# Sliding windows of a 2D image batch: another order of the loads, fewer split stores, and the last two stores back on the common queue

## The chip, the cores and the metric

The kernel runs on one core of one Trainium2 chip. The metric is the device time of one execution in microseconds; the figure for a kernel is the median of its runs. The profile is of one execution, and its times count from that execution's first instruction.

## The reference

The input `x` is a float32 array of 16 x 64 x 64 x 64 (batch, channel, height, width). For each of 15 x 15 window positions (8 x 8 windows, stride 4) the window of all channels is copied out. Nothing is computed; the output holds every input element about four times.

```python
for i in range(n_h):
    for j in range(n_w):
        h_start = i * stride
        w_start = j * stride
        result[:, i, j] = x[:, :, h_start:h_start + window_size, w_start:w_start + window_size].copy()
```

The output is 16 x 15 x 15 x 64 x 8 x 8 float32, 58.98 MB; the input is 16.78 MB. So 75.76 MB have to be moved.

## The kernel before, in words

**Layout.** The 128 partitions are (batch 16) x (channel half 2) x (height quarter 4). Each partition holds 32 channels (CL) of 16 rows (RB) by 64 columns, in one tile `L` (L45). A window position is a pair (j, s): j is the column position (15 of them), s one of four row slots within the partition's 16 rows (NSLOT). Because all four height quarters are worked at once, one pair (j, s) covers four rows of windows, or three for s = 3, where the quarter at the bottom has no window. There are 60 pairs, in `order` (L82), j outermost.

**Loads.** The channels are loaded in NCH = 4 parts of 8 channels (L49 to L54). Each part is four DMAs, one for each height quarter, alternating between the SP and ACT queues: 16 DMAs of 1,024 KB. The first half of a partition's channels is parts 0 and 1.

**Copies.** For each pair, `window` gathers the strided window of every partition into a contiguous store buffer. For s = 0 to 2 this is one copy on ACT (L111). For s = 3 the lower half of the window lies in the next partition, so DVE copies the upper four rows (L113) and fetches the lower four with a shuffle across partitions (L114).

**Store buffers.** `G` (L94) is a list of nine tiles, each of 18 / 2 units; a unit is a half window (16 channels, 512 KB over all partitions), a tile holds a whole one (1,024 KB). The counter `at` goes round the 18 units.

**Stores.** Each buffer leaves by an indirect DMA that POOL issues (L124): an index for each partition (`idx`, or `idx_last` for s = 3; `idx_h` and `idx_hlast` for half windows) gives the row of the output, and an index beyond the bound, for the bottom quarter at s = 3, is left out. All stores are declared independent of one another (`free`, L88). At most eight of them are under way: the next waits until the one eight places before it in the queue has landed. A copy into a tile waits until the store that last read the tile has landed.

**Order.** The first EARLY = 12 pairs are split: their first half (channels of parts 0 and 1) is copied and stored as soon as these parts are there (L136). Then second halves and whole windows alternate, two and two (L140 to L145), and whole windows follow (L146).

**The last two pairs.** The pairs in `order[-TAIL:]`, TAIL = 2, are stored by plain DMAs on the SP queue (L115 to L119), one for each height quarter: four for (14, 2), three for (14, 3), 256 KB each. Ahead of them the counter is set back by three tiles (L148, BACK = 3), so they use tiles again whose stores were issued last but two and last but one.

Of the kernel before, what the change touches and what calls it, by code (L numbers as in the profile page):

```python
# [1 line left out]

# [4 lines left out]


@with_exitstack  # L10
def kernel(
    ctx: ExitStack,
    tc: tile.TileContext,
    x: bass.AP,
    window_size: int,
    stride: int,
    out: bass.AP,
):
    nc = tc.nc
    P = nc.NUM_PARTITIONS  # L20

    B, C, H, W = x.shape
    Bo, NH, NW, Co, WSo, WSo2 = out.shape
    WS = int(window_size)
    ST = int(stride)
    assert Bo == B and Co == C and WSo == WS and WSo2 == WS

    f32 = mybir.dt.float32
    i32 = mybir.dt.int32
    ALU = mybir.AluOpType  # L30
    HQ = 4
    CH = P // (B * HQ)
    CL = C // CH
    RB = H // HQ
    NSLOT = RB // ST
    NWIN = NH * NW
    CFREE = CL * WS * WS
    assert HQ == 4 and CH == 2 and WS == 2 * ST

    lpool = ctx.enter_context(tc.tile_pool(name="lpool", bufs=1))  # L40
    ipool = ctx.enter_context(tc.tile_pool(name="ipool", bufs=1))
    gpool = ctx.enter_context(tc.tile_pool(name="gpool", bufs=1))


    L = lpool.tile([P, CL, RB, W], f32)  # L45
    x_v = x.rearrange("b (ch cl) (hq r) w -> hq (b ch) cl (r w)", ch=CH, hq=HQ)
    NCH = 4
    cw = CL // NCH
    for k in range(NCH):  # L49
        for q in range(HQ):  # L50
            (nc.sync, nc.scalar)[q % 2].dma_start(
                out=L[q::HQ, k * cw : (k + 1) * cw, :, :],
                in_=x_v[q, :, k * cw : (k + 1) * cw, :],
            )  # L54


    def itile(name):
        return ipool.tile([P, 1], i32, name=name)

    pi, tb, tq, tc_, idx, idx_last = (itile(n) for n in ("pi", "tb", "tq", "tc", "idx", "idx_last"))  # L60
    nc.gpsimd.iota(pi[:, :], pattern=[[0, 1]], base=0, channel_multiplier=1)  # L61
    nc.vector.tensor_scalar(out=tb[:, :], in0=pi[:, :], scalar1=3, scalar2=None, op0=ALU.logical_shift_right)  # L62
    nc.vector.tensor_scalar(out=tc_[:, :], in0=pi[:, :], scalar1=2, scalar2=1, op0=ALU.logical_shift_right, op1=ALU.bitwise_and)  # L63
    nc.vector.tensor_scalar(out=tq[:, :], in0=pi[:, :], scalar1=HQ - 1, scalar2=None, op0=ALU.bitwise_and)  # L64
    nc.vector.tensor_scalar(out=tb[:, :], in0=tb[:, :], scalar1=float(NWIN * CH), scalar2=None, op0=ALU.mult)  # L65
    nc.vector.tensor_tensor(out=tb[:, :], in0=tb[:, :], in1=tc_[:, :], op=ALU.add)  # L66
    nc.vector.tensor_scalar(out=tc_[:, :], in0=tq[:, :], scalar1=float(NSLOT * NW * CH), scalar2=None, op0=ALU.mult)  # L67
    nc.vector.tensor_tensor(out=idx[:, :], in0=tb[:, :], in1=tc_[:, :], op=ALU.add)  # L68

    nc.vector.tensor_scalar(out=tq[:, :], in0=tq[:, :], scalar1=float(HQ - 1), scalar2=float(2 * B * NWIN * CH), op0=ALU.is_equal, op1=ALU.mult)  # L70
    nc.vector.tensor_tensor(out=idx_last[:, :], in0=idx[:, :], in1=tq[:, :], op=ALU.add)  # L71


    HCL = CL // 2
    idx_h, idx_hlast = itile("idx_h"), itile("idx_hlast")
    for d, e in ((idx_h, idx), (idx_hlast, idx_last)):
        nc.vector.tensor_scalar(out=d[:, :], in0=e[:, :], scalar1=2.0, scalar2=None, op0=ALU.mult)  # L77
    o_v = out.rearrange("b i j (ch cl) r w -> (b i j ch) (cl r w)", ch=CH)
    o_h = out.rearrange("b i j (ch cl) r w -> (b i j ch) (cl r w)", ch=2 * CH)
    nxt = [min(p + 1, 31) for p in range(32)]  # L80

    order = [(j, s) for j in range(NW) for s in range(NSLOT)]  # L82


    TAIL, BACK = 2, 3
    o_q = out.rearrange("b i j (ch cl) r w -> i j b ch (cl r w)", ch=CH)

    def free(st):  # L88
        tc.declare_no_dep(st.ins, group="stores", reason="each store writes rows of its own")
        tc.add_to_no_dep_group("stores", st.ins)  # L90


    UNITS = 18
    G = [gpool.tile([P, 2 * HCL, WS, WS], f32, name=f"G{n}") for n in range(UNITS // 2)]  # L94
    at = 0

    def window(j, s, half):
        nonlocal at
        cols = slice(j * ST, j * ST + WS)
        last = s == NSLOT - 1  # L100
        if half is None:
            n, c0 = 2, 0
            at += at % 2
        else:
            n, c0 = 1, half * HCL
        u = at % UNITS
        at += n
        cs = slice(c0, c0 + n * HCL)
        g = G[u // 2][:, u % 2 * HCL : (u % 2 + n) * HCL, :, :]
        if not last:  # L110
            nc.scalar.copy(out=g, in_=L[:, cs, s * ST : s * ST + WS, cols])  # L111
        else:
            nc.vector.tensor_copy(out=g[:, :, 0:ST, :], in_=L[:, cs, s * ST : RB, cols])  # L113
            nc.vector.stream_shuffle(out=g[:, :, ST:WS, :], in_=L[:, cs, 0:ST, cols], mask=nxt)  # L114
        if (j, s) in order[-TAIL:]:  # L115
            g_q = g.rearrange("(m q) c r w -> q m (c r w)", q=HQ)
            for q in range(HQ - 1 if last else HQ):
                free(nc.sync.dma_start(out=o_q[q * NSLOT + s, j], in_=g_q[q]))
            return  # L119
        if half is None:  # L120
            o, ix = o_v, (idx_last if last else idx)
        else:
            o, ix = o_h, (idx_hlast if last else idx_h)
        st = nc.gpsimd.indirect_dma_start(  # L124
            out=o,
            out_offset=bass.IndirectOffsetOnAxis(ap=ix[:, 0:1], axis=0),
            in_=g.rearrange("p c r w -> p (c r w)"),
            in_offset=None,
            element_offset=(s * NW + j) * CH * CFREE + (half or 0) * HCL * WS * WS,
            bounds_check=B * NWIN * CH * (1 if half is None else 2) - 1,  # L130
            oob_is_err=False,
        )
        free(st)

    EARLY = 12
    for j, s in order[:EARLY]:  # L136
        window(j, s, 0)
    late = list(order[:EARLY])
    rest = list(order[EARLY:])
    while late:  # L140
        for w in late[:2]:
            window(*w, 1)
        for w in rest[:2]:
            window(*w, None)
        late, rest = late[2:], rest[2:]  # L145
    for w in rest[:-TAIL]:  # L146
        window(*w, None)
    at -= 2 * BACK  # L148
    for w in rest[-TAIL:]:
        window(*w, None)  # L150


# [1 line left out]
_INS = ['x', 'window_size', 'stride']  # L154
_OUTS = [((16, 15, 15, 64, 8, 8), 'float32')]

_NUMBERS = {'window_size': 8, 'stride': 4}


# [26 lines left out]
```

## Time and profile before

| | us |
|---|---|
| median of 3 runs | 193.19 |
| range of the runs | 192.94 to 193.51 |
| the profiled execution's own time | 193.19 |
| its span, first to last instruction | 191.4 |
| ACT busy | 86.2 (45%) |
| POOL busy | 68.0 (36%) |
| DVE busy | 30.4 (16%) |
| packets of the indirect stores, share of 16 DMA engines | 73.3% (57.15 MB) |
| packets of the SP queue (8 loads, 7 stores) | 13.8% (10.22 MB) |
| packets of the ACT queue (8 loads) | 11.1% (8.39 MB) |

The mean time of one instruction: 1,896 ns for an ACT copy of a whole window and 1,040 ns for a half; 694 and 1,280 ns for DVE's copy and shuffle of a whole window; some 965 ns for POOL's issue of a store. The busy time of POOL on a store is the issue alone; the bytes move afterwards. From issue to landing the profile gives a median of 18.4 us for whole windows and 14.1 us for half windows on POOL's queue, 4.2 us for SP's stores, and 21.1 and 19.8 us for the loads on SP's and ACT's queues. The DMA share of a stretch can read a little over 1 because packets overlap.

### The profile page before, as it was taken

To read this page: it belongs to the slowest core of one execution; us is meant where nothing else is said; L and a number is where in the kernel's file an instruction comes from. 1 tells how busy PE (TensorE), PEld (TensorE's weight loads), DVE (VectorE), ACT (ScalarE), POOL (GpSimd) and SP (SyncE) were. 2 spreads that over 40 slices of the span, in tenths; PEclk is the share of its full clock that TensorE was granted. 3 is DMA by queue.
4 is the path that set the end of the run, shared out by engine and by line. 5 is a ranking of instruction groups with operands and counts; after the bars stand their busy time and mean duration, and the time that the engine had idled before them with its cause. 6 is when DMAs were issued, how large, how long until landed. Compare 5 with 4: busy or idle time off the path is not lost.

```text
span 191.4 us, 479 instructions
## 1 busy us (share of the span) xinstructions
DVE 30.4 (16%) x65; ACT 86.2 (45%) x55; POOL 68.0 (36%) x75
## 2 busy tenths in 40 slices
DVE  2000050000232302301221031203030303000030
ACT  0000059400699876364566556565647473300300
POOL 0000028723367666464464343434444444400000
DMA  5999999999999999999999999999999999999785
GB/s 180 419 413 410 410 409 413 416 423 420 417 423 429 423 418 425 407 406 414 410 413 404 414 416 413 404 409 409 411 407 409 411 409 406 416 411 416 325 265 187
DMA packets 14772, 75.80 MB, mean 396 GB/s; under 512 B 2032, under 2 KB 2032, under 8 KB 9008
## 3 DMA queue, kind: packets, MB, share of 16 engines
q0 software_dynamic: 10080, 57.15, 73.3%
q1 hardware_dynamic: 2512, 10.22, 13.8%
q10 hardware_dynamic: 2176, 8.39, 11.1%
q14 instruction: 4, 0.03, 0.0%
HBM read 16.78 MB, written 62.65 MB: 415 GB/s over the span
## 4 chain that ended last, share of the span: by engine, by line
DMA 73%; issue 19%; ACT 2%; POOL 1%; DVE 1%; POOLq 0%; DVEq 0%; PEldq 0%; ACTq 0%
DMA out_dram<-G,idx 60%; DMA out_dram<-G,idx_h 13%; ACT G L111 2%; POOL out_dram L124 1%; DVE G L114 1%; DVE G L113 0%; POOLq L124 0%; POOL pi L61 0%; DVEq L113 0%; PEldq L181 0%; ACTq L111 0%
## 5 line engine op out<-in xcount | busy, mean ns | idle before, releaser
L111 ACT COPY G<-L 128x2048 f32<-128x2048 f32 (+1 forms) x54 | 84.9, 1611 | 69.1 <-DMA out_dram<-G,idx_last 25.1
L124 POOL DMA_INDIRECT out_dram<-G,idx x35 | 33.8, 966 | 45.9 <-DMA out_dram<-G,idx 41.7
L113 DVE COPY G<-L 128x1024 f32<-128x1024 f32 (+1 forms) x18 | 11.1, 614 | 152.1 <-DMA out_dram<-G,idx 76.5
L124 POOL DMA_INDIRECT out_dram<-G,idx_h x18 | 17.4, 964 | 13.9 <-DMA out_dram<-G,idx_hlast 4.8
L114 DVE STREAM_SHUFFLE G<-L 128x1024 f32<-128x1024 f32 (+1 forms) x18 | 19.6, 1091 | 0.0
L124 POOL DMA_INDIRECT out_dram<-G,idx_hlast x6 | 5.9, 989 | 27.8 <-DVE G L114 26.3
L124 POOL DMA_INDIRECT out_dram<-G,idx_last x11 | 10.6, 964 | 10.6 <-DVE G L114 5.8
L111 ACT ACT_TABLE_LOAD x1 | 1.3, 1283 | 25.9 <-DMA L<-in_x_dram 25.9
L62 DVE TENSOR_SCALAR tb<-pi 128x1 int32<-128x1 int32 x1 | 0.2, 154 | 1.0 <-POOL pi L61 1.0
L61 POOL IOTA pi<- 128x1 int32 x1 | 0.1, 119 | 0.4 <-PEq L181 0.4
L114 DVE LOAD_MASK_SELECT G<-L x18 | 0.2, 12 | 0.0
L167 POOL MEMSET const-float32-0.0<- 128x1 f32 x1 | 0.1, 98 | 0.2 <-issue 0.2
L66 DVE CUSTOM_DVE_ANT_0 tb<-tb,tc 128x2 uint16<-128x2 uint16 x1 | 0.2, 160 | 0.0
L68 DVE CUSTOM_DVE_ANT_0 idx<-tb,tc 128x2 uint16<-128x2 uint16 x1 | 0.2, 158 | 0.0
L67 DVE TENSOR_SCALAR tc<-tq 128x1 int32<-128x1 int32 x1 | 0.2, 153 | 0.0
L77 DVE TENSOR_SCALAR idx_hlast<-idx_last 128x1 int32<-128x1 int32 x1 | 0.2, 153 | 0.0
L77 DVE TENSOR_SCALAR idx_h<-idx 128x1 int32<-128x1 int32 x1 | 0.2, 154 | 0.0
L71 DVE CUSTOM_DVE_ANT_0 idx_last<-idx,tq 128x2 uint16<-128x2 uint16 x1 | 0.2, 153 | 0.0
L65 DVE TENSOR_SCALAR tb<-tb 128x1 int32<-128x1 int32 x1 | 0.2, 151 | 0.0
L70 DVE TENSOR_SCALAR tq<-tq 128x1 int32<-128x1 int32 x1 | 0.1, 147 | 0.0
L64 DVE TENSOR_SCALAR tq<-pi 128x1 int32<-128x1 int32 x1 | 0.1, 144 | 0.0
L63 DVE TENSOR_SCALAR tc<-pi 128x1 int32<-128x1 int32 x1 | 0.1, 143 | 0.0
(3 smaller groups left out, 0.3 us busy)
## 6 DMA issues: line engine op xcount, KB each, us to landing
L<-in_x_dram SPq DMA_DIRECT2D x8, 1024.0 KB, 21.1
L<-in_x_dram ACTq DMA_DIRECT2D x8, 1024.0 KB, 19.8
out_dram<-G SPq DMA_DIRECT2D x7, 256.0 KB, 4.2
out_dram<-G,idx POOLq DMA_INDIRECT x35, 18.4
out_dram<-G,idx_h POOLq DMA_INDIRECT x18, 14.1
out_dram<-G,idx_last POOLq DMA_INDIRECT x11, 18.4
out_dram<-G,idx_hlast POOLq DMA_INDIRECT x6, 11.9
```

Source lines behind the costliest of these rows:

```text
L61: nc.gpsimd.iota(pi[:, :], pattern=[[0, 1]], base=0, channel_multiplier=1)
L62: nc.vector.tensor_scalar(out=tb[:, :], in0=pi[:, :], scalar1=3, scalar2=None, op0=ALU.logical_shift_right)
L65: nc.vector.tensor_scalar(out=tb[:, :], in0=tb[:, :], scalar1=float(NWIN * CH), scalar2=None, op0=ALU.mult)
L66: nc.vector.tensor_tensor(out=tb[:, :], in0=tb[:, :], in1=tc_[:, :], op=ALU.add)
L67: nc.vector.tensor_scalar(out=tc_[:, :], in0=tq[:, :], scalar1=float(NSLOT * NW * CH), scalar2=None, op0=ALU.mult)
L68: nc.vector.tensor_tensor(out=idx[:, :], in0=tb[:, :], in1=tc_[:, :], op=ALU.add)
L71: nc.vector.tensor_tensor(out=idx_last[:, :], in0=idx[:, :], in1=tq[:, :], op=ALU.add)
L77: nc.vector.tensor_scalar(out=d[:, :], in0=e[:, :], scalar1=2.0, scalar2=None, op0=ALU.mult)
L111: nc.scalar.copy(out=g, in_=L[:, cs, s * ST : s * ST + WS, cols])
L113: nc.vector.tensor_copy(out=g[:, :, 0:ST, :], in_=L[:, cs, s * ST : RB, cols])
L114: nc.vector.stream_shuffle(out=g[:, :, ST:WS, :], in_=L[:, cs, 0:ST, cols], mask=nxt)
L124: st = nc.gpsimd.indirect_dma_start(out=o, out_offset=bass.IndirectOffsetOnAxis(ap=ix[:, 0:1], axis=0), in_=g.rearrange("p c r w -> p (c r ...
```

## The change

The four parts of the channels are loaded in the order 2, 0, 1, 3, so the first half of the channels (parts 0 and 1) comes second and third. EARLY is 8 in place of 12: eight pairs are split into halves, and four more pairs are stored whole. TAIL, BACK, the seven plain stores on SP and the setting back of the counter are gone: the last two pairs are stored by POOL's indirect DMAs like all others, from the tiles that are next in turn. What `free` did is written in its place.

```diff
-    for k in range(NCH):
+
+    for k in (2, 0, 1, 3):
         for q in range(HQ):
             (nc.sync, nc.scalar)[q % 2].dma_start(
...
-    TAIL, BACK = 2, 3
-    o_q = out.rearrange("b i j (ch cl) r w -> i j b ch (cl r w)", ch=CH)
-
-    def free(st):
-        tc.declare_no_dep(st.ins, group="stores", reason="each store writes rows of its own")
-        tc.add_to_no_dep_group("stores", st.ins)
-
...
-        if (j, s) in order[-TAIL:]:
-            g_q = g.rearrange("(m q) c r w -> q m (c r w)", q=HQ)
-            for q in range(HQ - 1 if last else HQ):
-                free(nc.sync.dma_start(out=o_q[q * NSLOT + s, j], in_=g_q[q]))
-            return
...
-        free(st)
+        tc.declare_no_dep(st.ins, group="stores", reason="each store writes rows of its own")
+        tc.add_to_no_dep_group("stores", st.ins)
 
-    EARLY = 12
+    EARLY = 8
     for j, s in order[:EARLY]:
         window(j, s, 0)
...
-    for w in rest[:-TAIL]:
-        window(*w, None)
-    at -= 2 * BACK
-    for w in rest[-TAIL:]:
+    for w in rest:
         window(*w, None)
```

## The prediction

> **What bounds the kernel now.** I read the page first: how busy the DMA engines are, and the chain that ended last.
>
> ```profile
> span 191.4 us, 479 instructions
> ...
> DMA  5999999999999999999999999999999999999785
> GB/s 180 419 413 410 410 409 413 416 423 420 417 423 429 423 418 425 407 406 414 410 413 404 414 416 413 404 409 409 411 407 409 411 409 406 416 411 416 325 265 187
> ...
> DMA 73%; issue 19%; ACT 2%; POOL 1%; DVE 1%; POOLq 0%; DVEq 0%; PEldq 0%; ACTq 0%
> ```
>
> No compute engine is over 45% busy, while the DMA engines are full from the second of the 40 slices to the 37th. The kernel moves bytes at 404 to 429 GB/s and is late only at its two ends. What matters is therefore (a) whether the DMA engines ever run out of work, (b) at what rate they move it, and (c) how the last bytes leave. I then asked for the rate by stage (columns: stretch, its length, busy time and number of instructions on DVE, ACT and POOL, clock, DMA share, GB/s).
>
> ```profile
> 4.00:25.00 21.00, 0.00 (x0) 0.00 (x0) 0.00 (x0) 1.00 1.02 412
> 30.00:49.00 19.00, 0.00 (x0) 5.80 (x7) 9.60 (x10) 1.00 1.03 419
> 50.00:60.00 10.00, 2.62 (x6) 10.00 (x9) 6.57 (x7) 1.00 1.03 423
> ...
> 100.00:160.00 60.00, 12.34 (x21) 34.15 (x18) 23.88 (x25) 1.00 1.01 410
> 160.00:179.50 19.50, 0.49 (x1) 4.08 (x3) 3.09 (x4) 1.00 1.01 414
> 179.50:182.00 2.50, 0.27 (x1) 1.61 (x1) 0.00 (x0) 1.00 0.51 213
> 182.00:189.50 7.50, 1.62 (x3) 0.00 (x0) 0.00 (x0) 1.00 0.87 282
> ```
>
> Loads alone run at 412, loads beside half-stores at 419, half-stores and the first whole ones at 423, whole stores alone at 410 to 414. From 179.5 us the rate halves and never recovers. The timeline there tells why, and the chain of waits gives the pace of the stores before it (start, length, what).
>
> ```profile
> 165.95 0.96 POOL L124 DMA_INDIRECT out_dram<-G,idx  x1 [1.50 <-DMA out_dram<-G,idx]
> 179.21 1.90 ACT L111 COPY G<-L 128x2048 f32<-128x2048 f32 x1 [14.52 <-DMA out_dram<-G,idx_last]
> 181.14 6.21 SPq L118 DMA_DIRECT2D out_dram<-G  x7
> 181.73 0.69 DVE L113 COPY G<-L 128x1024 f32<-128x1024 f32 x1 [21.24 <-DMA out_dram<-G,idx]
> ```
>
> ```profile
> 124.37 18.75 DMA out_dram<-G,idx
> ...
> 143.88 18.84 DMA out_dram<-G,idx
> ...
> 163.49 18.12 DMA out_dram<-G,idx
> ```
>
> POOL issues its last store at 165.95. The copy for the next-to-last window waits 14.52 us for a buffer, because the counter was set back by three tiles, onto a tile whose store is still queued; the last window waits 21.24 us in the same way. SP issues its seven plain stores from 181.14 on, when the queue of indirect stores is running dry. In the chain, each store is issued when the one eight before it lands. Landings are at 124.37 + 18.75 = 143.12, then 162.72, then 181.61: eight windows (six whole, two of three quarters, so 7.5 whole stores) take 19.60 and 18.89 us, or 2.61 and 2.52 us for one whole store, 1.96 and 1.89 us for a last row.
>
> **The change, part by part.**
>
> *The tail.* Removed: the setting back of the counter, and seven SP stores of 256 KB (1.84 MB in all). Added: two indirect stores on POOL, 0.96 us of issue each (L124). They take the next free tiles, so the copies no longer wait 14.52 and 21.24 us but, like every window before them, for the store nine back; and the issue waits for the store eight back. In the timeline the stores issued at 149.03 and 151.01 are those two; at 18.7 us to land and some 0.75 us to the next issue (162.72 to 163.49 in the chain) the new stores go out near 168.5 and 170.5, with more than ten microseconds of queue before them. So they simply follow in the queue. The store issued at 163.49 lands at 181.61; after it come the one of 165.95, the new whole one and the new last-row one: 2 x 2.52 + 1.89 = 6.93 us at the better pace, 2 x 2.61 + 1.96 = 7.18 at the worse, so the last byte lands at 188.5 to 188.8. Before, SP's last issue is at 186.2 and its median landing 4.2 us later, so 190.4. The tail is worth 1.6 to 1.9 us; I take 1.7, nearer the pace that held for most of the run. The close from the last landing to the end of the span (191.4 - 190.4 = 1.0 us) waits for all queues in both kernels and stays.
>
> The Trainium skill, in "DMA: Bandwidth & Descriptors", section "Issuing engine by pattern", sends a simple store to Sync and says HWDGE is generally faster; that speaks against this part. Here the plain stores got 282 GB/s (182 to 189.5) and the indirect ones 410 to 414, so the row disagrees for stores of 256 KB issued one after another. By the page the removal would cost, by the row it gains, and I go by the row.
>
> *The load order.* Sixteen load DMAs of 1,024 KB go out as before, on the same queues; only which part they carry changes. The first copies need parts 0 and 1, which in the old order are the first eight DMAs, landed when ACT's wait ends at 25.89; in the new order twelve are needed. Four more are 4.19 MB, at 412 GB/s 10.2 us: 36.1. The first store, 1.38 us after the loads in the old kernel (27.27 against 25.89), goes out at 37.5. This costs nothing only while loads keep the engines full. All loads alone would last 16.78 MB / 412 = 40.7 us from about 2.3, to 43; from about 39 the stores take a share. With loads running, POOL's waits for a free slot end at 40.23, 43.98 and 47.29, so a half-store (0.52 MB or 0.39) lands each 3.5 us: a third of the rate. The last 1.7 MB of loads then take some 6 us, to 45, in place of 49.6. Half-stores issued from 37.5 on at one per 1.27 us (31.22, 32.49, 33.76 in the timeline) are seven by then, 3.4 MB, of which 0.85 has gone: 2.5 MB are queued, 6 us of cover. The next supply: the second halves' copies start at 45, take 1.04 us each on ACT, and POOL stores them from 47.7 on. The cover of 6 us is over twice the 2.7 needed, so the hole is priced at nothing; with no cover it would be 2.7 plus about 2 us from issue to first bytes, some 4.7.
> What does cost is the rate: some 12 us that ran mixed at 419 now run as loads alone at 412, 12 x 7/412 = 0.2 us; from 0, if mixing only shifts what is moved when, to 0.4 if it is doubled by the slower start.
>
> *Eight split windows in place of twelve.* Four windows of 3.93 MB leave as four stores in place of eight, so POOL issues four fewer (3.9 us of an engine that is 36% busy, hidden under the DMA). The transfer: 3.93 MB at 423 is 9.3 us, at 410 it is 9.6; so 0 to 0.3 us lost. The first whole stores ran in the fast stage too, so I take 0.1. Copies on ACT and DVE shrink by their fixed part (two of 1.04 against one of 1.90), hidden.
>
> The same page's section "Bandwidth" asks for at least 1 MiB per DMA, by which dropping halves of 0.5 MB would gain. The stages here say 423 with halves and 410 without, so nothing is booked as a gain.
>
> *The buffers.* The list of nine tiles is the same text in both versions; nothing to cost. Declaring the stores independent moves into the function, with no instruction.
>
> **The sum.** 191.4 - 1.7 + 0.2 + 0.1 = 190.0 us of span. The profiled execution took 193.19 us, 1.8 over its span, and is itself the median of the three runs. 190.0 + 1.8 = 191.8 us. If paces and rates take their good ends, 191.4 - 1.9 + 1.8 = 191.3; at their bad ends, 191.4 - 1.6 + 0.4 + 0.3 + 1.8 = 192.3.
>
> **The rivals.**
> 1. *Slower: the pace of the stores falls.* The place is the long stage of whole stores from about 55 us to the end. Its cycle was 18.89 us once and 19.60 otherwise; at 423 GB/s 7.86 MB would take 18.6, so the pace already moves by a microsecond for reasons that the page doesn't show. The new stage starts some 10 us earlier and there are no other DMAs at its end to use engines that finish early: the halved rate at 179.5 shows that some finish well before others. If the cycle is 20.2 in place of 19.6, the 6.8 cycles from 55 to 188 add 4.1 us: 195.9. It decides, against the 1.4 us forecast, from 0.3 us a cycle on (2 us in all). For it: the rate did fall when halves ended. Against it: the bytes and their places are the same, and the last cycle was the fastest.
> 2. *No change.* If the spread of the engines' ends, at least the 2.5 us for which the rate was halved, is a fifth wider at the new last store (my choice of size), that is 0.5 us more; if the load order and the whole stores each cost their bad end too, 0.4 + 0.3, then 191.4 - 1.6 + 1.2 + 1.8 = 192.8.
> 3. *A hole after the loads.* If the first stores got no share of the engines before 45 us and were slow to start, the 4.7 us worked out above appear as a dip near 45 to 50 us: 191.8 + 4.7 = 196.5. Against it: in the old kernel stores landed beside the loads all the time, and seven or eight are queued.
> 4. *The reordering does more than it says:* the early stage without half-stores could be faster. If the whole-store cycle is 18.89 throughout, four cycles gain 0.7 each: 191.8 - 2.8 = 189.0. Nothing in the edit asks for it.
>
> **How the numbers follow.** Forecast 0.60 (191.3 to 192.3); slower pace 0.14; no change 0.12; hole 0.06; faster pace 0.08. A measurement of this kernel can tell 0.3%, 0.58 us, from no change: faster means below 192.6, slower above 193.8. Faster is 0.60 + 0.08 = 0.68, same 0.12, slower 0.20. The time is the likeliest case's, 191.8. The range reaches down to half of the faster pace, 190.2, and up through no change into the start of the slower pace, 194.3, leaving out the hole, the rest of that pace, and half of the fast case: about 2 in 10.
>
> **What would show it.** First POOL store near 37.5 us and loads' last wait ending near 45; DMA share at 1.0 through 40 to 55; POOL's last two stores issued near 168.5 and 170.5; the GB/s row above 400 to about 180 us and nothing from SP at the end; last landing near 189. Wrong if the share dips near 45 to 50, if the eight-store links of the chain grow past 19.9 us, or if the last store lands more than 20 us after its issue.

## The result and the profile after

The changed kernel takes 194.59 us (median of 6 runs, 194.38 to 194.76) against 193.37 us for the kernel before (median of 6); the ratio is 1.0066 with a 95% interval of 1.0053 to 1.0079. It is slower by 1.2 us where 1.4 us less had been forecast. The profiled execution took 194.45 us, with a span of 192.7 us.

The page of the changed kernel, the same rows as before:

```profile
span 192.7 us, 457 instructions
...
DMA  5999999999999999999999999999999999999950
GB/s 186 421 410 411 411 409 409 409 413 417 421 429 424 415 424 403 412 415 413 415 418 413 410 408 413 406 408 415 412 401 408 412 412 405 407 417 410 429 242 26
```

The DMA engines are full one slice longer than before (to the 38th), half busy in the 39th, and the last slice, 4.8 us long, moves next to nothing. So the bytes are out earlier and the kernel ends later. The rates by stage at the end (columns as in the table shown for the kernel before):

```profile
160.00:179.50 19.50, 2.40 (x4) 5.69 (x3) 5.06 (x6) 1.00 1.01 411
179.50:182.00 2.50, 0.00 (x0) 0.00 (x0) 0.00 (x0) 1.00 1.02 423
182.00:184.00 2.00, 0.00 (x0) 0.00 (x0) 0.00 (x0) 1.00 1.01 418
184.00:189.10 5.10, 0.00 (x0) 0.00 (x0) 0.00 (x0) 1.00 0.44 183
189.10:192.70 3.60, 0.00 (x0) 0.00 (x0) 0.00 (x0) 1.00 0.00 0
```

Full rate to 184, half the engines' work to 189.1, and then 3.6 us in which not a byte moves. Before, that last stretch was 1.0 us. The timeline of the new tail and of the new head (start, length, what, idle time before and what ended it):

```profile
36.06 1.28 ACT L104 ACT_TABLE_LOAD   x1 [36.06 <-DMA L<-in_x_dram]
...
37.46 1.12 POOL L112 DMA_INDIRECT out_dram<-G,idx_hlast  x1 [36.51 <-DVE G L107]
...
45.78 16.58 ACT L104 COPY G<-L 128x1024 f32<-128x1024 f32 x12 [2.65 <-DMA L<-in_x_dram]
```

```profile
169.38 0.98 POOL L112 DMA_INDIRECT out_dram<-G,idx  x1 [1.99 <-DMA out_dram<-G,idx]
...
171.19 0.97 POOL L112 DMA_INDIRECT out_dram<-G,idx_last  x1 [0.83 <-DVE G L107]
```

The first store goes out at 37.46, the loads' last wait ends at 45.78, POOL's last two stores are issued at 169.38 and 171.19; all of this is within 0.9 us of where the prediction had put it. The last store is 17.9 us under way, so it lands at 189.1, against 190.4 for SP's last store before.

What stands in the 3.6 us does not show on the page, whose tables leave out instructions that only wait. It shows when the trace is asked for the instructions of the launch line, where the program ends (L167 in the changed kernel, L181 in the old one). DRAIN is one of the instructions with which every engine's queue ends there. Columns: engine's queue, operation, count, shortest/median/longest in ns, first and last start. The changed kernel:

```profile
L167 POOLq DRAIN  x3: 40/108/20922, 171.0 to 192.4; - x3
L167 SPq DRAIN  x3: 7/7/7, 189.4 to 192.1; - x3
```

The kernel before:

```profile
L181 POOLq DRAIN  x3: 40/108/21658, 165.7 to 191.2; - x3
L181 SPq DRAIN  x3: 7/7/7, 190.6 to 190.9; - x3
```

The longest of POOL's three DRAINs is the first. It begins as the last store is issued and lasts 20.92 us in the changed kernel, from 171.0 to 191.9: it ends 2.8 us after the last store has landed, and the span 0.8 us later. SP, which waits for the landings before its own DRAIN, had reached that DRAIN at 189.4; ACT and DVE had ended theirs by 170.8, so POOL alone held the end. In the old kernel POOL's DRAIN ran from 165.7 to 187.4, until 2.9 us after POOL's last store had landed (issued at 165.95, 18.5 us under way, so 184.5). There SP's plain stores were still moving until 190.4, and it did not show. SP's own DRAIN takes 7 ns, and the old kernel closed 1.0 us after SP's last landing. What POOL does between the landing and the end of its DRAIN the trace does not tell.

### The profile page after: what moved, and what is told of

Same layout as the page of the kernel before. It is cut to its first block, busy times and chain, and to the rows that moved or that the text cites. A ratio compares the mean times of both kernels' runs of the same rounds, so it can differ in the third digit from the quotient of the medians.

```text
span 192.7 us, 457 instructions
## 1 busy us (share of the span) xinstructions
DVE 30.4 (16%) x62; ACT 86.2 (45%) x52; POOL 66.6 (35%) x73
## 4 chain that ended last, share of the span: by engine, by line
DMA 58%; issue 25%; ACT 3%; POOL 3%; POOLq 1%; ACTq 0%; PEldq 0%
DMA out_dram<-G,idx_last 47%; DMA out_dram<-G,idx 7%; DMA out_dram<-G,idx_h 4%; ACT G L104 3%; POOL out_dram L112 3%; POOLq L167 1%; POOLq L112 0%; POOL pi L62 0%; ACTq L104 0%; PEldq L167 0%
## 5 line engine op out<-in xcount | busy, mean ns | idle before, releaser
L104 ACT COPY G<-L 128x2048 f32<-128x2048 f32 (+1 forms) x51 | 84.9, 1695 | 45.3 <-DMA out_dram<-G,idx 17.9
L112 POOL DMA_INDIRECT out_dram<-G,idx x39 | 37.9, 972 | 51.1 <-DMA out_dram<-G,idx 47.3
L112 POOL DMA_INDIRECT out_dram<-G,idx_last x13 | 12.5, 965 | 12.8 <-DVE G L107 7.8
L112 POOL DMA_INDIRECT out_dram<-G,idx_hlast x4 | 4.0, 1006 | 37.4 <-DVE G L107 36.5
L112 POOL DMA_INDIRECT out_dram<-G,idx_h x12 | 11.8, 980 | 3.7 <-issue 2.4
```

The lines of the kernel that those rows point to most:

```text
L112: st = nc.gpsimd.indirect_dma_start(out=o, out_offset=bass.IndirectOffsetOnAxis(ap=ix[:, 0:1], axis=0), in_=g.rearrange("p c r w -> p (c r ...
```

## The experiments

Theory: POOL's queue closes (its long DRAIN ends) 2.8 to 2.9 us after its last store has landed, and some 0.8 us follow; after the last plain store on SP or ACT the span needs only 1.0 us. The old tail hid POOL's closing behind plain stores; the change brought it out. Rival: the two edits of the head cost the time. Further experiments asked what the old tail is bound by, and whether there is a better one. Their ratios are to runs of the kernel before on the same chip, with 95% intervals.

### The tail undone alone

```diff
-    TAIL, BACK = 2, 3
+    TAIL, BACK = 2, 0
...
-        if (j, s) in order[-TAIL:]:
+        if (j, s) in order[-TAIL:] and BACK:
```

> The kernel before with only its tail undone: the last two pairs go by POOL's indirect stores from the next tiles; old load order, twelve split pairs. Theory (closing of POOL): in the changed kernel POOL's last DRAIN ended 2.83 us after its last store landed (189.06 to 191.89), and the span 0.8 us after that, where the old kernel closed 1.0 us after SP's last landing. Then the last store lands here near 188.7, the span is 188.7 + 3.65 = 192.3 and the time 194.1, some 0.8 above before. Rival (head): the load order and the eight splits cost the time and the tail gains as forecast; then the span is 188.7 + 1.0 = 189.7 and the time 191.5.

Measured: 194.24 us against 193.27, ratio 1.0052 (1.0035 to 1.0069). The theory's 194.1 fits; the rival's 191.5 does not. The chain of this kernel ends in the same way as the changed one's:

```profile
151.11 18.87 DMA out_dram<-G,idx_last
...
170.53 1.19 POOLq L181
```

and its DRAIN is as long:

```profile
L181 POOLq DRAIN  x3: 40/108/21304, 170.5 to 192.3; - x3
```

The last store, issued at 170.75, is 18.1 us under way and lands at 188.8; the DRAIN ends at 191.8, the span at 192.6.

### The head alone

```diff
-    for k in range(NCH):
+    for k in (2, 0, 1, 3):
...
-    EARLY = 12
+    EARLY = 8
```

> The kernel before with only the head changed: load order 2, 0, 1, 3 and eight split pairs; the plain stores on SP and the setting back are kept. Theory (closing of POOL): the head is worth 0 to 0.4 us; time 193.3 to 193.8. Rival (head): the 2.8 us by which the changed kernel missed the forecast come from here; time near 196.

Measured: 193.43 us, ratio 1.0007 (0.9993 to 1.0021). Load order and eight splits together cost nothing that can be told from zero. With the run above, the tail carries the change: 1.0052 alone, 1.0066 with the head.

### Each edit of the head by itself

The first and the second hunk of the diff above, one at a time.

> The kernel before with the load order 2, 0, 1, 3 alone; twelve pairs split. Theory: 0.2 us from less mixing (0 to 0.4), first store near 37.5; but twelve half-stores at 1.27 us each now last to 52, past the end of the loads near 45, which costs nothing while the queue holds work; time 193.3 to 193.8. Rival (the two edits of the head cancel): this alone costs 0.6 us or more: 193.9 or above.

> The kernel before with eight split pairs and the old load order. Theory: 0 to 0.3 us from the transfer, plus what a short supply costs: eight half-stores from 27.3 on are issued by 37.3, the loads end near 49, so the stores have 3.5 MB against 22 us at a third of the rate (3 MB); little or no hole; time 193.2 to 193.8. Rival (the two edits of the head cancel): this alone gains or costs 0.6 us or more.

Measured: the load order alone 194.16 us, ratio 1.0054 (1.0035 to 1.0073); the eight splits alone 194.90 us, ratio 1.0088 (1.0065 to 1.0111). Here the rival held: each edit costs by itself, 0.9 and 1.6 us, and together they cost nothing. For the eight splits the stages show where (columns as above):

```profile
50.00:52.50 2.50, 2.44 (x6) 2.46 (x3) 1.14 (x1) 1.00 1.03 419
52.50:55.00 2.50, 0.40 (x1) 2.50 (x2) 1.89 (x3) 1.00 0.77 311
55.00:60.00 5.00, 1.30 (x3) 5.00 (x5) 3.26 (x5) 1.00 0.98 398
60.00:80.00 20.00, 3.92 (x6) 16.07 (x11) 14.32 (x15) 1.00 1.01 397
```

```profile
36.42 0.96 POOL L124 DMA_INDIRECT out_dram<-G,idx_h  x1 [0.30 <-issue]
50.04 3.79 ACT L111 COPY G<-L 128x1024 f32<-128x1024 f32 x3 [16.98 <-DMA L<-in_x_dram]
...
51.36 1.18 POOL L124 DMA_INDIRECT out_dram<-G,idx_h  x1 [13.98 <-ACT G L111]
```

With the old order the stores start at 27.4; the eighth and last half-store is issued at 36.42, the next copy can begin at 50.04 and the next store at 51.36. The queue runs short: the DMA share falls to 0.77. The kernel before moves 419 and 427 GB/s from 52.5 to 55 and from 55 to 60 us, so the hole costs some 0.41 MB, 1.0 us at 410 GB/s. From 60 to 80 us this kernel moves 397 GB/s at a full share, where the kernel before moves 419; that is another 1.1 us, and no run shows why. In the changed kernel the same eight half-stores start 10 us later and carry over the end of the loads, without a dip:

```profile
45.00:52.50 7.50, 3.18 (x6) 6.72 (x6) 5.73 (x6) 1.00 1.03 419
52.50:55.00 2.50, 0.00 (x0) 2.50 (x3) 1.89 (x3) 1.00 1.03 419
```

The dip is the prediction's third rival, the hole after the loads, in a combination that the change avoids. Why the load order alone costs 0.9 us is not settled: there is no hole, but its rate from 60 to 80 and from 80 to 100 us is 413 and 409 GB/s where the kernel before has 419 and 411, some 0.4 us of it. Why this cost does not show in the pair is not settled either.

### Plain stores early

```diff
-    TAIL, BACK = 2, 3
+    TAIL, BACK = 2, 0
```

> The kernel before with the counter not set back (BACK 0): the last two pairs still go by plain stores on SP, but from tiles that are free some 13 us earlier, so SP issues them near 166 to 171 beside POOL's queue. Theory (closing of POOL): the same bytes leave, POOL's last store now lands last, near 188.7, and its closing follows: span 192.3, time 194.1. Rival (late start): the old tail lost time because the plain stores started late; with them early the last landing is near 188.7 and the close 1.0: time 191.5.

Measured: 197.41 us, ratio 1.0228 (1.0206 to 1.0250), worse than either expected. The plain stores did go out from 167.5 on and landed by 187.3, and POOL's last store landed last and closed the kernel: issued at 166.24, it took 25.1 us and landed at 191.4, and

```profile
L181 POOLq DRAIN  x3: 40/108/28262, 166.0 to 194.8; - x3
```

the DRAIN ended at 166.0 + 28.3 = 194.3, 2.9 us later. So the closing is where the theory had it; what it missed is that the two kinds of store side by side run slower:

```profile
168.00:170.00 2.00, 1.86 (x3) 0.00 (x0) 0.00 (x0) 1.00 1.02 410
170.00:175.00 5.00, 0.04 (x1) 0.00 (x0) 0.00 (x0) 1.00 1.01 356
175.00:180.00 5.00, 0.00 (x0) 0.00 (x0) 0.00 (x0) 1.00 1.01 351
```

The DMA share stays at 1.01 while the rate falls from 410 to 351 GB/s: each byte holds the engines longer. What in a plain store of 32 partitions makes it so was not tried.

### Other plain tails

The plain stores dealt to two queues; the counter set back by four tiles; both; and only one pair left to plain stores, on two queues:

```diff
-                free(nc.sync.dma_start(out=o_q[q * NSLOT + s, j], in_=g_q[q]))
+                free((nc.sync, nc.scalar)[q % 2].dma_start(out=o_q[q * NSLOT + s, j], in_=g_q[q]))
```

```diff
-    TAIL, BACK = 2, 3
+    TAIL, BACK = 2, 4
```

```diff
-    TAIL, BACK = 2, 3
+    TAIL, BACK = 1, 3
```

> The kernel before with its seven plain stores dealt to SP and ACT in turn (four and three). Theory (closing of POOL is hidden in the old tail, and the old tail is bound by SP's issue: seven issues in 6.2 us, 0.89 us each): the stores are issued in some 3.5 us, the last lands near 188, POOL's closing ends at 187.4 and stays hidden; span 189.0, time 190.8, below both kernels. Rival (the plain stores are bound by the DMA engines, half of which still drain the queue): last landing 190 to 190.4, time 193.

> The kernel before with the counter set back by four tiles in place of three, so that the last copies wait for stores that land one place earlier (some 1.9 us) and SP starts near 179.2 in place of 181.1. Theory (closing of POOL hidden, tail bound by SP's issue of 0.89 us a store): SP's last landing moves from 190.4 to 188.6, POOL's last store is delayed a little by sharing the engines (to 185.5), its closing ends at 188.4 and stays hidden; span 189.6, time 191.5. Rival (plain stores beside the queue slow both, as where the counter was not set back: 351 GB/s at a full DMA share): no gain, time 193.0 to 193.6.

> The same with the seven plain stores dealt to SP and ACT in turn. Theory (closing hidden while the plain stores end 2.1 us or more after POOL's last landing): with two queues the last plain store lands near 188, POOL's last near 186 and its closing near 189: the closing starts to show; span 189.8, time 191.6. Rival (sharing slows both): 192.7 as with two queues and three tiles, or worse.

> The kernel before with only the last pair (14, 3) left to plain stores (TAIL 1), dealt to SP and ACT; (14, 2) goes by POOL. The plain stores are issued near 183.7 and land near 187.5, POOL's last store lands near 187.2. Theory (closing of POOL: the span ends 3.65 us after POOL's last landing or 1.0 us after the last plain one, whichever is later): 187.2 + 3.65 = 190.9, time 192.7, although all bytes are out 2 us earlier than with two pairs on two queues. Rival (what counts is the last landing of any queue): 187.5 + 1.0 = 188.5, time 190.3.

Measured:

| kernel | us | ratio (95%) |
|---|---|---|
| two queues | 192.67 | 0.9978 (0.9964 to 0.9992) |
| set back by four | 192.98 | 0.9994 (0.9977 to 1.0010) |
| set back by four, two queues | 193.50 | 1.0019 (1.0003 to 1.0035) |
| one pair, two queues | 193.15 | 1.0012 (0.9994 to 1.0031) |

Two queues are the one version here that beats both kernels, by 0.2%, less than a quarter of what was expected of it. The issue of the stores on it:

```profile
L118 SPq DMA_DIRECT2D out_dram<-G x4: 598/1158/1346, 181.3 to 184.9; - x4
L118 ACTq DMA_DIRECT2D out_dram<-G x3: 615/1291/1670, 181.3 to 183.8; - x3
```

A median issue that took 0.82 us on SP alone takes 1.16 and 1.29 us when two queues issue side by side, so seven issues end at 186.2 in place of 187.3, and the last store lands at 189.8, not near 188. The old tail was bound by SP's issue only in part. Starting 1.8 us earlier (179.31 in place of 181.14) brought nothing that can be measured: SP's seven issues took 7.8 us in place of 6.2, POOL's last store landed 0.8 us later than before, and the last plain one 0.5 us earlier. With two queues it cost: the plain stores took a median of 8.5 us to land, 5.5 without the earlier start. Both times agree with the rival, that plain stores beside the queue slow both. With one pair, POOL's closing and the plain stores end together: the plain ones landed at 189.8 (not at 187.5 as expected), POOL's last at 187.4, its DRAIN ended at 190.3 and the span at 191.1. This one told the theories apart poorly, since 189.8 + 1.0 = 190.8 is nearly the same.

The eleven profiled executions together (us; the DRAIN's start and length are from the rows of the launch line, and a landing is a store's issue plus its time to landing):

| kernel | POOL's last landing | its DRAIN ends | last plain landing | span |
|---|---|---|---|---|
| before | 184.5 | 187.4 | 190.4 | 191.4 |
| after | 189.1 | 191.9 | none | 192.7 |
| tail undone | 188.8 | 191.8 | none | 192.6 |
| head alone | 185.7 | 188.4 | 191.3 | 192.3 |
| load order alone | 185.9 | 188.8 | 191.3 | 192.2 |
| eight splits alone | 187.3 | 190.1 | 192.4 | 193.4 |
| not set back | 191.4 | 194.3 | 187.3 | 195.1 |
| two queues | 185.0 | 187.9 | 189.8 | 190.8 |
| set back by four | 185.3 | 188.2 | 189.9 | 190.8 |
| set back by four, two queues | 185.8 | 188.7 | 190.8 | 191.8 |
| one pair, two queues | 187.4 | 190.3 | 189.8 | 191.1 |

In all eleven the DRAIN ends 2.7 to 3.0 us after POOL's last landing, and the span ends 0.8 us after the DRAIN or 1.0 us after the last plain landing, whichever is later (where the columns give 0.9, it is their rounding).

## Why the prediction was wrong

*The tail's bytes: right.* The prediction had the last landing move from 190.4 to 188.5 to 188.8, and by 0.3 us less far with the head's cost: 189.0. It landed at 189.1. The new stores were issued 0.7 to 0.9 us later than forecast, which cost nothing with 18 us of queue ahead of them. The chain of the changed kernel has the pace that the sum used:

```profile
131.93 18.78 DMA out_dram<-G,idx_last
...
151.48 18.94 DMA out_dram<-G,idx_last
...
170.97 1.19 POOLq L167
```

Landings at 150.71, 170.42 and, for the store of 171.19, at 189.1: 19.71 and 18.6 us for eight windows. The chain's last piece is POOL's queue itself, where the old one ended in DVE's copy for the plain stores.

*The close: the step that failed.* "The close from the last landing to the end of the span (191.4 - 190.4 = 1.0 us) waits for all queues in both kernels and stays." It did not stay: it is 3.6 us when the last landing is POOL's. That is 2.6 us; the forecast span of 190.0 plus 2.6 is 192.6, and 192.7 was measured. The 1.0 us had been read from a kernel in which the queue that closes slowly was done early. Its cost was in the trace of before, 2.9 us between POOL's last landing and the end of its DRAIN, hidden behind 6 us of plain stores; it belongs to what those stores covered, and nothing on the page said so.

*The slower rival: wrong in kind.* It put a slower outcome down to the stores' pace. From 100 to 160 us the rate is 410 GB/s in both kernels; the row of the changed one:

```profile
100.00:160.00 60.00, 12.79 (x21) 34.15 (x18) 23.91 (x25) 1.00 1.01 410
```

*The load order and the splits: right together, wrong apart.* Their sum, 0.3 us with bounds of 0 to 0.7, agrees with the 1.0007 (0.9993 to 1.0021) of the head alone. But they had been priced one by one at 0.2 and 0.1 us, and one by one they cost 0.9 and 1.6: that the sum came out was luck. The price of "eight splits" was worked out for the bytes alone; that it also shortens the supply during the loads, and that the later start pays for this, was seen only for the pair.

*The skill's advice.* The Trainium skill, "DMA: Bandwidth & Descriptors", "Issuing engine by pattern", would have left the simple stores on Sync. The prediction set the row of 282 GB/s against it. The row was right on the rate, and the page right on the outcome, though by a cost that this section does not state. "VectorE: DVE Perf Modes", "The DRAIN you can't avoid", gives about 12 ns, on all five engines, for the DRAINs that the runtime puts around a kernel. The DRAINs here stand on the program's own launch line, of which that section does not speak: SP's 7 ns are near its figure, and POOL's 20.9 us, ending 2.8 us after its last store landed, are not.

## What to carry to other kernels

A closing cost belongs to the queue that finishes last, so when an edit changes which queue that is, the old kernel's close is no price for the new one: ask the trace for the instructions at the program's last line, engine by engine, and see which ends were covered. Indirect stores may fill the stream, but here the last few microseconds were better left to queues that close quickly, even at two thirds of the rate. Two edits that change one supply, when the work begins and how much of it there is, have to be priced together.

## What the runs showed of the hardware

POOL's queue closed 2.7 to 3.0 us after its last indirect store had landed in eleven of eleven executions. The DMA engines don't end together: in the changed kernel they work at a share of 0.44 from 184.0 to 189.1, after 1.01 and 1.02 up to there, and of the 16 signals by which the trace records the last store's landing eight come from 184.3 to 184.9 and eight from 188.6 to 189.1. In the old kernel, where the plain stores start at 181.1, the share is 0.87 from 182.0 to 189.5. And plain stores of 256 KB beside indirect ones hold the engines at a full share while the rate falls from 410 to 351 GB/s; neither of these last two was followed further.
